# Sums of the first MLP weights' blocks: accumulating DMAs in DRAM in place of additions on VectorE

## The chip, the cores and the metric

The kernel runs on one core of a Trainium2 chip. The core has five engines, each with a queue of its own: TensorE (PE in the profile, with PEld for its weight loads), VectorE (DVE), ScalarE (ACT), GpSimd (POOL) and SyncE (SP). Transfers (DMAs) are issued from the queues of SP, ACT and POOL and are carried out by 16 DMA engines that all of them share. The metric is the device time of one execution in microseconds. The kernel before takes 1538.17 us, the median of three runs (1535.3 to 1539.74).

## The reference

The reference is one inference step of a backbone of two layers over 640 tokens: 512 latent tokens (`x_sample`) and 128 context tokens (`x_prompt`), of width 1024. All is float32. Each layer is

```
shift1, scale1, gate1, shift2, scale2, gate2 = split(mod)      # mod = silu(c) @ w_ada[l] + b_ada[l]
y = mixer(rmsnorm(x, norm1) * (1 + scale1) + shift1)           # one input projection, four head groups, one output projection
x = x + gate1 * y
h = rmsnorm(x, norm2) * (1 + scale2) + shift2
x = x + gate2 * (square(relu(h @ w1)) @ w2)                    # w1: 1024 x 4096, w2: 4096 x 1024
```

The four head groups are a short gated convolution, a chunked spatial-gating MLP, a latent attention and a windowed attention with sinks. A last RMSNorm ends it. The outputs are both groups of tokens and the context tokens' new cache entries of each layer. The change concerns `h @ w1` of the second layer.

## The kernel before

**Layout.** The activations lie feature-major in `x` (128 partitions, 8 k-tiles, 640 tokens). Tokens are worked on in two halves of 384 and 256 columns (`HALVES`). A weight arrives as a unit of 128 x 1024 float32 (512 KB) in a buffer of the pool `raw` (three buffers); ScalarE casts it to a high half and VectorE subtracts to get the low half, both in one tile `hl` (four buffers). `mm3` (L248 to L250) makes each product from three matmuls: high by high, high by low, low by high. `load_unit` (L235 to L240) is this sequence; with `pool=True` POOL makes the low half, which is used in layer 0's first projections and for the first four MLP units.

**Start.** `first_modulate` (L302) loads x from ScalarE's queue (four DMAs, L133) and natural-layout parts of `w_ada` as `adan` from SP's queue: eight tiles at L311 and, after these are used, four at L327. It ends with `late_consts`, which loads `vec` of layer 1 and `fn` (L143, L144). A `Norm` adds up squares, has POOL raise them to the power -1/2 (L295), and the result scales x. The rest of `w_ada` is streamed as `adaw` (`ada_tile`, L168 to L174) between other work through the whole of layer 0; the products with the conditioning vectors are made on VectorE.

**Mixer.** `tm_block` makes three token-major projections from units `raw<-in_wt`. The cached keys `cc` (L620) are loaded in the code behind all three. POOL's part in the mixer is the power of the row norms (L482) and the scaling of attention probabilities (L731, L968).

**MLP of layer 0.** 32 units of w1 and 32 of w2. `two_plain(j)` (L1232) makes four 128-row tiles of the hidden layer: per unit and half, 24 matmuls, a ReLU on ScalarE into `rr`, a square into `u`, a second square on POOL into `rq` (L1145), and on VectorE the low half of `u` (L1146). The buffers of `rr` and `rq` are five of the pool `pp` in all; the results of PE go through four single PSUM banks (`bank`). `mlp2(j)` (L1251) then multiplies by the w2 units, 12 matmuls per tile and half, and `gate_add` (L428) adds into x. The loop runs j = 0 to 7, `two_plain(j + 1)` ahead of `mlp2(j)`. After each unit of `mlp2` comes one `ada_steps(1)` as long as there are `adaw` tiles left.

**MLP of layer 1.** Here `h @ w1` is made by blocks (`Pair`): the units are taken in pairs, and for each pair a 2 x 2 block product of seven multiplications takes the place of eight. Pairs 0 and 1 are done plainly. For pairs 2 to 15, `full(p)` (L1223) calls `load` (L1149 to L1153), which fetches the two raw units r1 and r2 on SP's queue; `w1` splits r1; `w2` (L1163 to L1173) first makes four sums of blocks on VectorE, of 128 x 512 elements each, into the tiles `s23` and `s14` (tag `s`, two buffers in the pool `me`), and splits those and the last block of r2:

```
nc.vector.tensor_add(s14[:, 0], r2[:, 0], r2[:, 1])       # L1167
nc.vector.tensor_add(s23[:, 0], r1[:, 0], s14[:, 0])      # L1168
nc.vector.tensor_add(s23[:, 1], r1[:, 0], r2[:, 0])       # L1169
nc.vector.tensor_add(s14[:, 1], r1[:, 1], s23[:, 0])      # L1170
```

`first` and `rest` make the seven products (PSUM tiles `qa`, `qb`, `qcd`), each four blocks of three matmuls of 320 columns. The loop alternates `full` twice with one `mlp2`.

**Order.** The code is written as a sequence of tile operations. A planner orders each engine's queue when the program is built: an instruction may be placed ahead of earlier ones in the code if its operands, its buffers and its engine are free by the planner's own estimate of times. Once built, each queue runs strictly in order, and an instruction that waits holds everything behind it on its queue. The planner also sets all waits on semaphores.

Of the kernel before, what the change touches and what calls it, by code (L numbers as in the profile page):

```python
# [10 lines left out]
F32 = mybir.dt.float32  # L11
# [3 lines left out]
ALU = mybir.AluOpType  # L15
# [30 lines left out]
U_W1 = 9  # L46
# [10 lines left out]
def step_kernel(ctx, tc, xT, wf, wt, wt3, wo1, wo2, wq, wkvs, wada, wnat, wnat2, vec, rows, fnorm, cvec, cache, kpec,  # L57
                masks, rope_s, rope_q, rope_k, o_y, o_ckv, o_kpe, o_k, o_v):
    nc = tc.nc
# [11 lines left out]
    s2 = ctx.enter_context(tc.tile_pool(name="s2", bufs=2, space=PSUM))  # L71
# [9 lines left out]

    def close_phase():
        phase.pop("stack").close()

    uid = [0]

    def nm(s):
        uid[0] += 1
        return f"{s}_{uid[0]}"
# [9 lines left out]
    def bank2(s="bk2"):  # L99
        return s2.tile([128, 2, 512], F32, tag="s2", name=nm(s))  # L100
# [4 lines left out]
    def tb(shape, s, dt=F32R):  # L105
        return pool_b.tile(shape, dt, tag="b", name=nm(s))
# [10 lines left out]
    def tmp2(shape, s):  # L117
        return t2.tile(shape, F32, tag="t2", name=nm(s))
# [49 lines left out]
    def ada_tile(l, ct, pool=None):  # L168

        raw = pool([128, D], "adaw", F32) if pool else rawp.tile([128, D], F32, tag="raw", name=nm("adaw"))  # L170
        nc.sync.dma_start(out=raw, in_=wada[l, ct])
        junk = bank2("junk").rearrange("p a b -> p (a b)")
        for g in range(2):
            nc.vector.tensor_tensor_reduce(  # L174
                out=raw if g else junk, in0=raw, in1=cb[:, g, :], op0=ALU.mult, op1=ALU.add, scale=1.0,
                scalar=vecs[l][:, V_BADA + ct:V_BADA + ct + 1], accum_out=mods[l][g][:, ct:ct + 1])
        v, k = divmod(ct, KT)
        if v in (1, 4):
            gain(l, v // 4, k, 1)

    def gain(l, n, k, w):
        base, c0 = (V_N1, V_N2)[n], (KT, 4 * KT)[n] + k
        for g in range(2):
            nc.vector.scalar_tensor_tensor(
                out=gains[l][g][n][:, k:k + w], in0=mods[l][g][:, c0:c0 + w], scalar=1.0,
                in1=vecs[l][:, base + k:base + k + w], op0=ALU.add, op1=ALU.mult)

    class AdaRows:
# [6 lines left out]
        def step(self, k, raw):  # L195
            w = 128 * self.nk
            for v in range(2):
                nc.tensor.matmul(self.ps[0:2, v, :], lhsT=cs[:, :, k], rhs=raw[:, w * v:w * v + w],
                                 start=(k == 0 and (v == 0 or self.nk == 4)),
                                 stop=(k == KT - 1 and (v == 1 or self.nk == 4)))  # L200
# [27 lines left out]
    def ada_steps(n, pool=None):  # L228
        for _ in range(n):
            t = next(ada_it, None)  # L230
            if t is not None:
                ada_tile(*t, pool)


    def load_unit(src, n=1024, pool=False):  # L235
        raw = rawp.tile([128, 1024], F32, tag="raw", name=nm("raw"))
        nc.sync.dma_start(out=raw[:, :n], in_=src)
        hl = hlp.tile([128, 2, 1024], F32R, tag="hl", name=nm("hl"))
        nc.scalar.copy(hl[:, 0, :n], raw[:, :n])  # L239
        (nc.gpsimd if pool else nc.vector).tensor_sub(hl[:, 1, :n], raw[:, :n], f(hl[:, 0, :n]))  # L240
        return hl
# [15 lines left out]
    class Norm:  # L257
# [6 lines left out]
        def add(self, k, t0, n, pool=False):  # L264
            if k == 0:
                nc.scalar.activation(self.s[:, t0:t0 + n], x[:, k, t0:t0 + n], AF.Square)
                return
            sq = tmp2([128, 384], "sq")
            nc.scalar.activation(sq[:, :n], x[:, k, t0:t0 + n], AF.Square)  # L269
            (nc.gpsimd if pool else nc.vector).tensor_add(self.s[:, t0:t0 + n], self.s[:, t0:t0 + n], sq[:, :n])  # L270
# [165 lines left out]
    def layer(l, h, next_norm, nxt):  # L436
# [138 lines left out]
        ws = load_unit(wkvs[l, :, 512:1024], 512)  # L575
        wsH, wsL = (ws[:, s, 0:512].rearrange("p (h q) -> p h q", h=4) for s in range(2))
        for hd in range(4):
# [5 lines left out]
                out=u_t[:, :, d0:d0 + 64], in0=ps[:, :320].rearrange("p (t d) -> p t d", t=5),  # L583
# [501 lines left out]
        blocks = l == DEPTH - 1  # L1085
# [29 lines left out]
        me = phase.get("me")  # L1115

        class Pair:
# [5 lines left out]
            def __init__(self, p, u=None):  # L1123
                self.p = p
                pool = (lambda: me.tile([128, 2, TOK], F32R, tag="u", bufs=2, name=nm("u"))) if p % 3 == 0 \
                    else (lambda: tb([128, 2, TOK], "u"))
                self.u = u or [pool(), pool()]
                self.r, self.q = [None] * 2, [None] * 2
# [19 lines left out]
            def load(self):  # L1148
                self.raw = []  # L1149
                for i in range(2):  # L1150
                    raw = rawp.tile([128, 2, 512], F32, tag="raw", name=nm("raw"))
                    nc.sync.dma_start(out=raw, in_=wf[l, U_W1 + 2 * self.p + i].rearrange("p (a b) -> p a b", a=2))
                    self.raw.append(raw)  # L1153

            def hl(self, src, n=2):
                t = hlp.tile([128, 2, 2, 512], F32R, tag="hl", name=nm("hl"))
                split(t[:, 0, :n], t[:, 1, :n], src)
                return t
# [2 lines left out]
                self.wa = self.hl(self.raw[0])  # L1161

            def w2(self):  # L1163
                r1, r2 = self.raw
                s23 = me.tile([128, 2, 512], F32, tag="s", bufs=2, name=nm("s"))
                s14 = me.tile([128, 2, 512], F32, tag="s", bufs=2, name=nm("s"))
                nc.vector.tensor_add(s14[:, 0], r2[:, 0], r2[:, 1])  # L1167
                nc.vector.tensor_add(s23[:, 0], r1[:, 0], s14[:, 0])  # L1168
                nc.vector.tensor_add(s23[:, 1], r1[:, 0], r2[:, 0])  # L1169
                nc.vector.tensor_add(s14[:, 1], r1[:, 1], s23[:, 0])  # L1170
                self.ws23 = self.hl(s23)
                self.ws14 = self.hl(s14)
                self.w22 = self.hl(r2[:, 1:2], 1)  # L1173

            def mul(self, ps, w, i, op, start):
                for s in range(4):
# [74 lines left out]
        def mlp2(j, ut):  # L1251
            if j < 7:
                for i in range(4):
                    u = load_unit(wf[l, U_W2 + 4 * j + i])
                    for m in (2 * i, 2 * i + 1):
                        for half in range(2):
                            mlp2_tile(ut, u, m, half, None)
                    if l == 0:
                        ada_steps(1)
            else:  # L1260
                us = [load_unit(wf[l, U_W2 + 4 * j + i]) for i in range(4)]
                for m in range(8):
                    mlp2_tile(ut, us[m // 2], m, 0, next_norm)
                for m in range(8):
                    mlp2_tile(ut, us[m // 2], m, 1, next_norm)
                    if m >= 2:
                        nxt.step(0, m - 2)
                for half, k in ((0, 6), (0, 7)) + tuple((1, k) for k in range(KT)):
                    nxt.step(half, k)

        head = [Pair(p, None if blocks else [ta([128, 2, TOK], "u") for _ in range(2)]) for p in range(2)]
        ws = [load_unit(wf[l, U_W1 + i], pool=True) for i in range(4)]
# [181 lines left out]
```

## Time and profile before

| | |
|---|---|
| median of three runs | 1538.17 us (1535.3 to 1539.74) |
| profiled execution: device time, span | 1542.1 us, 1540.2 us |
| PE, PEld busy | 1477.7 us, 1418.2 us |
| DVE, ACT, POOL busy | 1129.9, 668.4, 242.9 us |
| mean granted clock of PE | 0.978 |
| DMA, mean over the span | 104 GB/s (160.22 MB) |

The span runs from the first to the last instruction of one profiled execution; its device time is a little longer. A busy time is the sum of an engine's instructions with overlaps counted once; a busy share is the average of stages that differ. The granted clock is given as a share of the full 2.4 GHz.

### The profile page before, as it was taken

The numbers are of one execution on the slowest core, as the hardware profiler recorded it, in microseconds if no ns is written. First come the engines' busy times: TensorE is split into PE (matmuls) and PEld (weight loads), VectorE is DVE, ScalarE is ACT, GpSimd is POOL, SyncE is SP. The second block draws the span as 40 slices with busy tenths as digits, with TensorE's granted clock in tenths as the row PEclk, the third lists the DMA queues.
The fourth block names the chain that finished last, engine by engine and source line by source line (L and its number), as shares of the span: only waits on it lengthen the run. The fifth ranks groups of instructions, "written<-read, shape, count | busy, mean of one in ns | idle before, by whom it ended". The sixth has DMA issues, their size and how long they took to land.

```text
span 1540.2 us, 25201 instructions
## 1 busy us (share of the span) xinstructions
PE 1477.7 (96%) x9716; PEld 1418.2 (92%) x9716; DVE 1129.9 (73%) x2210; ACT 668.4 (43%) x1400; POOL 242.9 (16%) x245
## 2 busy tenths in 40 slices
PE   6899999989999999999999999999999999999997
PEld 3798988889999999999999989898999999999996
DVE  5988877869978778776457666687886676566655
ACT  3544556744322322322236545675745244334422
POOL 2132103243210110110120120132300000000002
PEclk9899999999999999999999999999999999999999
DMA  8544321333654445444211411111223223222211
GB/s 312 202 134 139 99 67 35 102 101 100 204 161 155 151 139 163 151 150 138 80 49 57 128 43 35 36 49 45 83 69 96 69 83 96 62 76 96 84 55 69
DMA packets 50103, 160.22 MB, mean 104 GB/s; under 512 B 6208, under 2 KB 10304, under 8 KB 49984
## 3 DMA queue, kind: packets, MB, share of 16 engines
q1 hardware_dynamic: 48320, 154.68, 31.3%
q10 hardware_dynamic: 1664, 3.93, 0.7%
q8 instruction: 77, 1.26, 0.3%
q14 instruction: 42, 0.34, 0.1%
HBM read 155.55 MB, written 3.05 MB: 103 GB/s over the span
## 4 chain that ended last, share of the span: by engine, by line
PE 77%; DVE 10%; ACT 5%; issue 3%; POOL 1%; DMA 1%; POOLq 0%; DVEq 0%; ACTq 0%
PE w L250 13%; PE w L249 13%; PE w L248 13%; PE qcd L248 2%; PE fm L248 2%; PE qcd L250 2%; PE qcd L249 2%; PE fm L250 2%; PE fm L249 2%; PE out L248 2%; PE tm L249 2%; PE tm L248 2%; PE tm L250 2%; PE out L250 2%; PE out L249 2%
## 5 line engine op out<-in xcount | busy, mean ns | idle before, releaser
L248 PE MATMUL w<-u,hl 128*128 128x384 f32 (+1 forms) x1024 | 317.4, 310 | 5.7 <-DVE x L428 3.4
L249 PE MATMUL w<-u,hl 128*128 128x384 f32 (+1 forms) x1024 | 317.3, 310 | 0.7 <-DVE u L1198 0.7
L250 PE MATMUL w<-u,hl 128*128 128x384 f32 (+1 forms) x1024 | 317.1, 310 | 0.4 <-DVE hl L240 0.4
L239 ACT CAST hl<-raw 128x1024 fp32r<-128x1024 f32 (+3 forms) x176 | 170.6, 972 | 261.7 <-PE w L250 156.2
L240 DVE TENSOR_TENSOR hl<-raw,hl 128x1024 fp32r<-128x1024 f32 (+3 forms) x156 | 183.2, 1177 | 53.0 <-ACT hl L239 52.4
L428 DVE SCALAR_TENSOR_TENSOR x<-w,mod,x 128x128 f32<-128x128 f32 (+1 forms) x384 | 155.0, 434 | 73.1 <-PE w L250 71.8
L248 PEld LDWEIGHTS w<-u,hl 128*128 128x128 f32 x1024 | 194.6, 190 | 6.5 <-DVE x L428 3.6
L249 PEld LDWEIGHTS w<-u,hl 128*128 128x128 f32 x1024 | 194.8, 190 | 1.0 <-DVE u L1198 1.0
L250 PEld LDWEIGHTS w<-u,hl 128*128 128x128 f32 x1024 | 194.6, 190 | 0.6 <-DVE hl L240 0.6
L249 PE MATMUL w<-h,hl 128*128 128x384 f32 (+1 forms) x576 | 179.2, 313 | 3.6 <-DVE h L369 3.6
L250 PE MATMUL w<-h,hl 128*128 128x384 f32 (+1 forms) x576 | 179.4, 312 | 0.0
L248 PE MATMUL w<-h,hl 128*128 128x384 f32 (+1 forms) x576 | 179.0, 312 | 0.0
L174 DVE CUSTOM_DVE_ANT_0 junk<-adaw,cb,vec 128x1024 f32<-128x1024 f32 x84 | 110.5, 1317 | 28.2 <-DMA adaw<-in_wada 28.0
L270 POOL TENSOR_TENSOR ss<-ss,sq 128x384 f32<-128x384 f32 (+1 forms) x40 | 37.3, 932 | 504.7 <-ACT sq L269 503.9
L174 DVE CUSTOM_DVE_ANT_0 adaw<-adaw,cb,vec 128x1024 f32<-128x1024 f32 x84 | 114.2, 1359 | 1.1
L249 PEld LDWEIGHTS w<-h,hl 128*128 128x128 f32 x576 | 110.3, 192 | 4.8 <-DVE h L369 4.8
L1145 POOL TENSOR_TENSOR rq<-rr 128x384 f32<-128x384 f32 (+1 forms) x64 | 61.9, 969 | 334.2 <-ACT rr L1140 310.3
L248 PEld LDWEIGHTS w<-h,hl 128*128 128x128 f32 x576 | 110.5, 192 | 0.0
L250 PEld LDWEIGHTS w<-h,hl 128*128 128x128 f32 x576 | 110.3, 192 | 0.0
L248 PE MATMUL fm<-h,hl 128*128 128x256 f32 (+1 forms) x288 | 93.4, 324 | 2.1 <-DVE u L582 2.1
L249 PE MATMUL fm<-h,hl 128*128 128x256 f32 (+1 forms) x288 | 90.7, 315 | 0.0
L250 PE MATMUL fm<-h,hl 128*128 128x256 f32 (+1 forms) x288 | 90.6, 315 | 0.0
(329 smaller groups left out, 3404.6 us busy)
## 6 DMA issues: line engine op xcount, KB each, us to landing
raw<-in_wf SPq DMA_DIRECT2D x146, 512.0 KB, 3.5
adaw<-in_wada SPq DMA_DIRECT2D x84, 512.0 KB, 3.6
raw<-in_wo SPq DMA_DIRECT2D x24, 384.0 KB, 3.0
adan<-in_wnat SPq DMA_DIRECT2D x12, 512.0 KB, 8.3
raw<-in_wt SPq DMA_DIRECT2D x16, 384.0 KB, 3.3
x<-in_xT ACTq DMA_DIRECT2D x4, 640.0 KB, 7.2
raw<-in_wt SPq DMA_DIRECT2D x8, 288.0 KB, 3.0
raw<-in_wo SPq DMA_DIRECT2D x4, 512.0 KB, 3.6
```

Of the source, the lines that this page charges most:

```text
L174: nc.vector.tensor_tensor_reduce(out=raw if g else junk, in0=raw, in1=cb[:, g, :], op0=ALU.mult, op1=ALU.add, scale=1.0, scalar=vecs[l][:, ...
L239: nc.scalar.copy(hl[:, 0, :n], raw[:, :n])
L240: (nc.gpsimd if pool else nc.vector).tensor_sub(hl[:, 1, :n], raw[:, :n], f(hl[:, 0, :n]))
L248: nc.tensor.matmul(out, lhsT=lhs[0], rhs=rhs[0], start=start, stop=False, skip_group_check=more)
L249: nc.tensor.matmul(out, lhsT=lhs[0], rhs=rhs[1], start=False, stop=False, skip_group_check=more)
L250: nc.tensor.matmul(out, lhsT=lhs[1], rhs=rhs[0], start=False, stop=stop, skip_group_check=more)
L270: (nc.gpsimd if pool else nc.vector).tensor_add(self.s[:, t0:t0 + n], self.s[:, t0:t0 + n], sq[:, :n])
L428: nc.vector.scalar_tensor_tensor(out=x[:, m, t0:t0 + n], in0=ps[:, t0 - b0:t0 - b0 + n], scalar=mods[l][g][:, gate + m:gate + m + 1], in1= ...
L1145: nc.gpsimd.tensor_mul(q, r, r)
```

## The change

A class `WeightSums` makes the four sums of each pair in DRAM. Seven chunks of two pairs each (pairs 2 to 15) get two DRAM tiles, `ws23` and `ws14`. For a chunk, four plain DMAs from ScalarE's queue copy blocks of the weights into the tiles (lag 0), and four accumulating DMAs from POOL's queue add blocks or finished sums to them, one step later each (lags 1 to 3). Each of these 56 DMAs carries two blocks of 128 x 512, 512 KB. `step` is called behind each unit of `mlp2` in layer 0 from j = 4 on: 12 calls, of which ten have something to do. `Pair.load` in layer 1 then fetches the whole of r1, only the second half of r2, and the two sums into the `s` tiles, all on SP's queue; the four `tensor_add` of `w2` go.

```diff
+    dram = ctx.enter_context(tc.tile_pool(name="ws", bufs=1, space=bass.MemoryType.DRAM))
...
+    class WeightSums:
+        def __init__(self, l, c0, n):
+            self.l, self.c0, self.n, self.t = l, c0, n, 0
+            self.s23 = {}
+            self.s14 = {}
+
+        def of(self, p):
+            c, i = divmod(p, 2)
+            return self.s23[c][i], self.s14[c][i]
+
+        def step(self):
+            def blocks(c):
+                u = U_W1 + 4 * c
+                w = wf[self.l, u:u + 4].rearrange("(p i) q (a b) -> i a p q b", i=2, a=2)
+                return w[0, 0], w[0, 1], w[1, 0], w[1, 1]
+
+            def add(out, src):
+                nc.gpsimd.dma_start(out=out, in_=src, accum_op=ALU.add)
+
+            t = self.t
+            self.t += 1
+            for lag in (3, 2, 1, 0):
+                c = self.c0 + t - lag
+                if not self.c0 <= c < self.c0 + self.n:
+                    continue
+                a11, a12, a21, a22 = blocks(c)
+                if lag == 0:
+                    self.s23[c] = dram.tile([2, 128, 2, 512], F32, name=nm("ws23"))
+                    self.s14[c] = dram.tile([2, 128, 2, 512], F32, name=nm("ws14"))
+                s2, s3 = (self.s23[c][:, :, z, :] for z in range(2))
+                s1, s4 = (self.s14[c][:, :, z, :] for z in range(2))
+                if lag == 0:
+                    for out, src in ((s1, a21), (s3, a11), (s2, a11), (s4, a12)):
+                        nc.scalar.dma_start(out=out, in_=src)
+                elif lag == 1:
+                    add(s1, a22)
+                    add(s3, a21)
+                elif lag == 2:
+                    add(s2, s1)
+                else:
+                    add(s4, s2)
+
+    wsums = {1: WeightSums(1, 1, 7)}
...
@@ class Pair: def load(self) @@
-                    nc.sync.dma_start(out=raw, in_=wf[l, U_W1 + 2 * self.p + i].rearrange("p (a b) -> p a b", a=2))
+                    w = wf[l, U_W1 + 2 * self.p + i].rearrange("p (a b) -> p a b", a=2)
+                    nc.sync.dma_start(out=raw[:, i:], in_=w[:, i:])
                     self.raw.append(raw)
+                self.s = []
+                for src in wsums[l].of(self.p):
+                    t = me.tile([128, 2, 512], F32, tag="s", bufs=2, name=nm("s"))
+                    nc.sync.dma_start(out=t, in_=src)
+                    self.s.append(t)
...
             def w2(self):
-                r1, r2 = self.raw
-                s23 = me.tile([128, 2, 512], F32, tag="s", bufs=2, name=nm("s"))
-                s14 = me.tile([128, 2, 512], F32, tag="s", bufs=2, name=nm("s"))
-                nc.vector.tensor_add(s14[:, 0], r2[:, 0], r2[:, 1])
-                nc.vector.tensor_add(s23[:, 0], r1[:, 0], s14[:, 0])
-                nc.vector.tensor_add(s23[:, 1], r1[:, 0], r2[:, 0])
-                nc.vector.tensor_add(s14[:, 1], r1[:, 1], s23[:, 0])
+                s23, s14 = self.s
                 self.ws23 = self.hl(s23)
                 self.ws14 = self.hl(s14)
-                self.w22 = self.hl(r2[:, 1:2], 1)
+                self.w22 = self.hl(self.raw[1][:, 1:2], 1)
...
@@ def mlp2(j, ut): in the loop over i @@
                     if l == 0:
                         ada_steps(1)
+                        if 4 * j + i >= 16:
+                            wsums[1].step()
```

## Rows read from the trace of the kernel before

**Rows 1.** The page's first two parts, whole span

```profile
span 1540.2 us, 25201 instructions
...
PE 1477.7 (96%) x9716; PEld 1418.2 (92%) x9716; DVE 1129.9 (73%) x2210; ACT 668.4 (43%) x1400; POOL 242.9 (16%) x245
...
PEclk9899999999999999999999999999999999999999
DMA  8544321333654445444211411111223223222211
```

**Rows 2.** Windows: start:end, length, busy PE, PEld, DVE, ACT, POOL, clock, DMA, GB/s

```profile
0.00:20.00 20.00, 9.71 (x53) 9.22 (x54) 7.22 (x20) 9.99 (x23) 2.27 (x9) 0.93 0.93 360
20.00:120.00 100.00, 87.04 (x448) 67.66 (x446) 88.00 (x152) 46.23 (x119) 30.11 (x17) 0.93 0.54 183
...
640.00:670.00 30.00, 30.00 (x205) 30.00 (x204) 26.39 (x55) 4.35 (x5) 0.00 (x0) 1.00 0.45 143
...
1240.00:1293.00 53.00, 53.00 (x361) 52.62 (x360) 34.83 (x58) 20.57 (x28) 0.00 (x0) 1.00 0.26 80
```

**Rows 3.** Chain of waits, layer 1's MLP: start, length, what

```profile
1229.09 0.31 PE qcd L248
...
1282.27 0.31 PE qcd L248
```

**Rows 4.** Timeline of POOL, layer 0's MLP: start, length, instruction, idle before it

```profile
615.24 0.83 POOL L1145 TENSOR_TENSOR rq<-rr 128x384 f32<-128x384 f32 x1 [31.40 <-ACT rr L1140]
...
671.48 0.83 POOL L1145 TENSOR_TENSOR rq<-rr 128x384 f32<-128x384 f32 x1 [31.81 <-ACT rr L1140]
...
727.72 0.83 POOL L1145 TENSOR_TENSOR rq<-rr 128x384 f32<-128x384 f32 x1 [31.81 <-ACT rr L1140]
```

**Rows 5.** Groups by line, layer 1's MLP: count, busy us, mean ns, idle before

```profile
L248 PEld LDWEIGHTS qcd<-h,hl 128*128 128x128 f32 x112 | 21.0, 188 | 2.9 <-DVE rr L1213 1.1 <-DVE rr L1215 0.2
...
L1167 DVE TENSOR_TENSOR s<-raw 128x512 f32<-128x512 f32 x14 | 9.6, 688 | 2.1 <-DMA raw<-in_wf 2.0
...
L1170 DVE TENSOR_TENSOR s<-raw,s 128x512 f32<-128x512 f32 x14 | 9.5, 681 | 0.0
```

**Rows 6.** Who waited for whom, layer 1's MLP: us in total, times, longest

```profile
ACT hl L253 <- PE w L250: 132.8, 27, 6.0
...
DVE s L1167 <- DMA raw<-in_wf: 2.0, 3, 1.2
```

**Rows 7.** DMA issues over the span: count, KB each, us from issue to landing

```profile
raw<-in_wf SPq DMA_DIRECT2D x146, 512.0 KB, 3.5
...
adan<-in_wnat SPq DMA_DIRECT2D x12, 512.0 KB, 8.3
...
cs<-in_cvec SPq DMA_DIRECT2D x1, 8.0 KB, 2.6
```

**Rows 8.** Timeline of SP's queue, start of the kernel

```profile
13.70 0.33 SPq L143 DMA_DIRECT2D vec<-in_vec  x1
14.98 0.33 SPq L144 DMA_DIRECT2D fn<-in_fnorm  x1
...
38.56 3.96 SPq L327 DMA_DIRECT2D adan<-in_wnat  x4
...
53.55 0.65 SPq L620 DMA_DIRECT2D cc<-in_cache  x1
```

**Rows 9.** Waits of SP's queue in 0 to 60 us; ScalarE's queue, timeline

```profile
SPq L311 <- DMA x<-in_xT: 1.7, 1, 1.7
...
SPq L143 <- DMA adan<-in_wnat: 1.0, 1, 1.0
...
3.38 0.33 ACTq L133 DMA_DIRECT2D x<-in_xT  x1
```

**Rows 10.** Timeline of POOL, start of the kernel

```profile
16.53 1.55 POOL L295 TENSOR_TENSOR nst<-nst,mhalf 128x3 f32<-128x3 f32 x2 [15.23 <-DVE nst L293]
25.10 6.79 POOL L240 TENSOR_TENSOR hl<-raw,hl 128x768 fp32r<-128x768 f32 x3 [7.02 <-ACT hl L239]
```

## The prediction

> **What bounds the kernel now.** Read the page's first two parts before anything else. The span is 1540.2 us, and TensorE (PE) is busy for 1477.7 us of it, at a granted clock that is full in nearly every slice [rows 1]. So only work that feeds PE late can move the time. The windows by stage come next. In layer 1's MLP, where the removed additions run, PE is busy for all 53.00 us of a stretch of 53 us, at clock 1.00, while VectorE (DVE) is busy for 34.8 and the DMA engines for 0.26. In layer 0's MLP PE is full too (30.00 of 30 us), with the DMA engines at 0.45. The start is different: in the first 20 us PE is busy for 9.7 us and the DMA engines are 0.93 full, and from 20 to 120 us PE has 87 of 100 us with the DMA engines at 0.54 [rows 2]. There the loads set the pace.
>
> Is there something to win in layer 1's MLP? The chain of waits passes the same matmul of two successive rounds at 1229.09 and 1282.27: 53.18 us for 360 matmuls (two pairs of 7 x 12, and 192 of the second product), 147.7 ns each [rows 3]. In layer 0 the POOL multiplications recur every 56.24 us, for 384 matmuls of the same mean width: 146.5 ns [rows 4]. The two differ by 1.2 ns, so a round of layer 1 loses at most 360 x 1.2 = 0.45 us to everything that holds PE, and seven rounds lose 3 us.
>
> **The change part by part.** The profiled run took 1542.1 us, 1.9 more than its span; that is 3.9 above the median of 1538.2. I add to 1542.1 and take 3.9 off at the end.
>
> *Removed:* four additions in each of 14 pairs, 688 to 681 ns each [rows 5], 56 x 0.68 = 38 us of VectorE. They lie beside a full PE. PE's weight loads waited 2.9 us in all before the product that needs VectorE's sums, 1.3 us of it put down to VectorE [rows 5]. Gain: between 0 and 3 us; I take 1, the row nearest to it. What is late next is PE itself.
>
> *Loads in layer 1:* a pair fetches two sums of 512 KB and 256 KB less of the raw blocks, 0.75 MB more. At the 387 GB/s of the first 20 us (360 at a share of 0.93 [rows 2]) that is 2 us of DMA engines in 26.6 us, on a share of 0.26. The casts that read them are held by PE giving back the hl buffers, 132.8 us in all, whereas the waits for raw blocks sum to 2.0 us [rows 6]. Each s buffer comes free one pair ahead of its next use. Cost 0; without this cover it would be one landing of 3.5 us [rows 7] in each of 14 pairs, 49 us.
>
> *The new transfers:* seven chunks, each of four plain copies from ScalarE's (ACT) queue and four accumulating ones from POOL's: 28 and 28, each 512 KB within DRAM. No row shows such a transfer. A plain load of that size takes 1.35 us of all engines (0.524 MB at 387 GB/s) or 1.65 us by the rate of layer 0's MLP (143 GB/s at 0.45, so 318). An accumulating transfer may cost the same, or twice that, since it fetches two operands: 28 copies 38 to 46 us, 28 additions 38 to 92 us of engines.
>
> *When they run.* The copies read only an input and write DRAM that nothing else uses, so nothing holds them back to layer 0's MLP. The planner issues such transfers early. The loads of vec, fn and cc, written behind the whole first modulation (cc even behind three projections), go out at 13.70, 14.98 and 53.55 us, while the second adan loads, written earlier, wait for a buffer until 38.56 [rows 8]. I expect the copies at the front of ScalarE's queue, behind the four loads of x, in the stretch where PE waits for loads.
>
> Transfers of different queues also wait for one another there. SyncE's (SP) load of adan waits 1.7 us for a load of x that ScalarE issued, and vec 1.0 us for adan, though they share no data [rows 9]. The fourth load of x goes out only at 3.38 us [rows 9], when cs, one of the first transfers, has just had its 2.6 us to landing [rows 7]; I read this as a fixed number in flight over both queues. So the copies take places from the loads. If the two alternate, 28 copies pass together with 28 loads, 56 x 1.35 = 76 us, and what the loads had moved by then is 14.7 MB. Before, the loads had moved 7.2 MB in 20 us and went on at 183 GB/s [rows 2], which makes 14.7 MB at 20 + 7.5/0.183 = 61 us; all loads are late by 15 us at the end of that stretch. Bounds: 0 (copies placed behind the loads) and 46 us (all ahead of them). I take 15.
>
> *POOL.* A waiting addition holds POOL's queue, and behind it stand the norm's power (16.53 us), the weights' low halves of layer 0's projections (25.10 on, 6.79 us for three) and later the attention's scalings [rows 10]; PE waits for all of these. The order is fixed in advance, so each wait that lasts longer than planned is passed on. Bounds: 0 (POOL is busy only 30 of 100 us, and additions may fall into its gaps [rows 2]) and 28 x 8.3 = 232 us (each one waiting out a landing as long as adan's at the start [rows 7]). I take one ordinary landing of 3.5 us [rows 7] per chunk, for the two copies that the chunk's first additions wait for: 7 x 3.5 = 24.5 us. POOL also writes out these transfers; no row shows that, and I put it within the same bounds.
>
> *ScalarE's issue* of 28 copies: 0.33 us each by the row of the fourth x load [rows 9], 9 us beside gaps of an engine that is busy 46 of 100 us. Cost 0 to 9 us; I take 0.
>
> Sum: 1542.1 - 1 + 15 + 24.5 = 1580.6; less 3.9, **1577 us**. Its own range takes 0 to 46 for the loads and about 10 to 60 for POOL: 1548 to 1640.
>
> **The rivals.** *Program place.* The transfers stay in layer 0's last MLP rounds. POOL's multiplications of the round at 727.72 then stand behind the additions of the step before [rows 4]. Their waits need 28 copies and 21 additions, 49 transfers; with 0.55 of the engines free, one per 1.65/0.55 = 3.0 us, that ends 147 us after the first step at 640, at 787. PE can run on for six half tiles (five rr/rq buffers hold three results, four PSUM banks four more), 6 x 56.24/16 = 21 us, to 749. So 38 us are lost: 1542.1 + 38 - 1 - 3.9 = 1575. For it: the steps are written there. Against: rows 8.
>
> *Two engines.* The blocks' outermost dimension is 2. If a transfer is shared out by it, it runs on two of 16 engines: 0.524 MB at 387/16 x 2 = 48 GB/s is 10.8 us, and at 318 it is 13.2. The 28 copies from one queue then last 300 to 370 us, and each addition that the planner set too early holds POOL until its own. If POOL stands for half of that, 150 to 185 us are lost, at full length 300 to 370: 1542 + 168 - 4 = 1706 typically, 1908 at worst. If the planner reckons with it, nothing is lost but the loads' share on two engines. Against it in the profile: nothing, as every row here has the 128 partitions outermost.
> The Trainium skill ("DMA: Bandwidth & Descriptors", section "Rules for kernel authors", row "Use all 16 engines") states just this: an outermost dimension below 16 confines the transfer to at most that many engines. By that rule the sum is this rival's, and no run here shows it.
>
> *Hidden.* The additions fall into POOL's gaps and the copies behind the loads; what remains is the gain: 1533 to 1540, typically 1537, not slower. It decides for this if POOL never waits longer than planned and fewer than about four loads of the start are overtaken (4 x 1.35 = 5 us). For it: 1540 us of DMA engines with a low mean share, and sums needed only from about 1130 us on. Against: rows 9.
>
> **How the numbers follow.** A measurement of this kernel tells 0.3%, 4.6 us, from no change. Forecast (early, 1577) 0.40; program place (1575) 0.12; two engines (about 1706) 0.23; hidden 0.25, of which 0.05 is faster by over 4.6 us, which the bound of 3 us hardly allows, and 0.20 within it. Slower takes 0.40 + 0.12 + 0.23 = 0.75, of which some 0.03 would stay within 4.6 us. That gives 0.05, 0.23, 0.72. The range reaches from the hidden case's 1535 to 1740, past the typical case of two engines; outside stay its long half (0.10 to 0.12) and 0.03 below.
>
> **What would show it.** Early copies: ScalarE's queue shows 28 DMA issues ahead of 100 us, and first loads that land later than 8.3 us. Program place: they stand after 610 us, and PE has a gap near 749. Two engines: the copies take over 10 us each, with the mean DMA share low. POOL's hold: POOL's waits name DMA on the new tiles, ahead of L240, L482 or L1145. Layer 1's rounds should last 52.7 to 53.2 us. The prediction is wrong if PE has no new gap ahead of 1100 us, or if layer 1's MLP waits for the s tiles.

## The result and the profile after

The changed kernel took 1821.7 us (median of 4; 1819.9 to 1822.2) against 1538.7 us for the kernel before on the same chip: a ratio of 1.1833, 95% interval 1.1806 to 1.1861. The forecast was 1577 us with a range of 1535 to 1740; the sign was right, the size far off. One execution of a kernel below (k16) ran at a granted clock of 0.594 throughout and took 2418.3 us; its median leaves that one out.

The page's first three parts of the changed kernel; the counterparts are [rows 1]:

```profile
span 1820.4 us, 25325 instructions
...
PE 1537.5 (84%) x9716; PEld 1464.6 (80%) x9716; DVE 1101.2 (60%) x2154; ACT 667.4 (37%) x1400; POOL 280.0 (15%) x273
...
PEclk7679686876679899999999999999999999999999
DMA  6354565333433245454444212211121333333221
...
q0 software_dynamic: 32704, 14.88, 5.8%
q10 hardware_dynamic: 8888, 18.61, 2.7%
```

TensorE executes the same 9716 matmuls; they are busy for 59.8 us longer, as the granted clock is low in the first third (0.64 to 0.78 in the windows below, between the levels of 1.2 and 2.4 GHz), where PE has gaps. VectorE has 56 instructions fewer, the removed additions. The DMA engines are nowhere near full: the new queue q0 (POOL's, the 28 accumulating transfers) fills 5.8% of them and q10 (ScalarE's) 2.7%. A DMA share adds up the times of packets, so it can pass 1.

The windows (columns as in [rows 2]) say where the time went:

```profile
0.00:20.00 20.00, 5.73 (x32) 5.57 (x32) 2.83 (x9) 7.20 (x16) 0.73 (x7) 0.95 0.93 358
20.00:120.00 100.00, 29.75 (x96) 10.84 (x96) 36.88 (x65) 9.29 (x16) 14.33 (x9) 0.64 0.47 142
120.00:340.00 220.00, 145.42 (x729) 134.48 (x730) 99.42 (x202) 60.96 (x165) 49.71 (x41) 0.78 0.51 128
340.00:620.00 280.00, 184.14 (x1018) 164.65 (x1018) 133.61 (x301) 100.78 (x248) 59.28 (x55) 0.76 0.36 90
620.00:1100.00 480.00, 473.38 (x3185) 471.55 (x3185) 365.00 (x652) 142.49 (x245) 83.09 (x82) 0.99 0.42 134
```

From 20 to 120 us PE has 29.8 us of work instead of 87.0 [rows 2]; up to 620 us it stays starved, with a DMA share of 0.36 to 0.51. From 620 us on it is full again. The POOL multiplications of layer 0's MLP fix the border. The first and the last in the trace of before, then here:

```profile
358.98 0.83 POOL L1145 TENSOR_TENSOR rq<-rr 128x384 f32<-128x384 f32 x1 [2.93 <-ACT rr L1140]
...
751.53 0.61 POOL L1145 TENSOR_TENSOR rq<-rr 128x256 f32<-128x256 f32 x1 [1.93 <-ACT rr L1140]
...
639.46 0.83 POOL L1195 TENSOR_TENSOR rq<-rr 128x384 f32<-128x384 f32 x1 [3.06 <-ACT rr L1190]
...
1032.07 0.62 POOL L1195 TENSOR_TENSOR rq<-rr 128x256 f32<-128x256 f32 x1 [1.93 <-ACT rr L1190]
```

The first is 280.5 us late, and so is the last. So the whole loss lies ahead of layer 0's MLP, in the start and layer 0's mixer, and none where the additions are written (that MLP's last rounds) or where the sums are used: in layer 1's MLP the matmul of [rows 3] recurs every 53.2 us, as before.

```profile
1456.49 0.30 PE qcd L298
...
1509.68 0.30 PE qcd L298
```

Who held it, in 0 to 640 us (us in total, times, longest):

```profile
POOL ws L257 <- DMA ws<-in_wf: 291.8, 20, 57.5
POOL ws L257 <- DMA ws<-ws: 81.6, 6, 16.6
...
SPq L287 <- DMA ws<-in_wf: 46.6, 3, 26.0
```

L257 is the accumulating transfer, ws the sums in DRAM. POOL stands in front of them for 373 us in 26 waits: 241 us for ScalarE's copies (15 waits) and 132 for earlier additions (11). SP's load of weights (L287) waits for them as well. The chain of waits, 0 to 620 us, has "DMA ws<-in_wf 24.7%; issue 9.8%", together 214 us of 620 ("DMA ws<-ws" adds 2.4%); before, "issue" (time in which an engine waits for nothing that the profile shows) is 4.1% there and no such DMA exists. A stretch of it (start, length, what):

```profile
204.45 18.29 DMA ws<-in_wf
222.74 0.35 issue
223.08 31.54 DMA ws<-in_wf
254.62 0.29 issue
254.91 14.73 DMA ws<-ws
```

Three waits for transfers of 512 KB, 64.6 us, with next to nothing between. The page's list of DMA issues gives the median landings:

```profile
ws<-in_wf POOLq DMA_DIRECT2D x14, 512.0 KB, 27.7
ws<-ws POOLq DMA_DIRECT2D x14, 512.0 KB, 11.8
```

The copies on ScalarE's queue by the view of line 273 (length of the issue in ns, min/median/max; first and last start):

```profile
L273 ACTq DMA_DIRECT2D ws<-in_wf x28: 600/606/13678, 12.1 to 484.6; - x28
```

### The profile page after: what moved, and what is told of

Its sections match the earlier page's. It is cut to its first block, busy times and chain, and to the rows that moved or that the text cites. A ratio compares the mean times of both kernels' runs of the same rounds, so it can differ in the third digit from the quotient of the medians.

```text
span 1820.4 us, 25325 instructions
## 1 busy us (share of the span) xinstructions
PE 1537.5 (84%) x9716; PEld 1464.6 (80%) x9716; DVE 1101.2 (60%) x2154; ACT 667.4 (37%) x1400; POOL 280.0 (15%) x273
## 4 chain that ended last, share of the span: by engine, by line
PE 63%; DMA 11%; DVE 9%; issue 5%; ACT 4%; POOL 2%; ACTq 1%; POOLq 0%; DVEq 0%
PE w L300 11%; PE w L299 11%; PE w L298 11%; DMA ws<-in_wf 8%; PE qcd L298 2%; PE qcd L300 2%; PE qcd L299 2%; PE out L298 2%; PE fm L298 2%; PE out L300 2%; PE out L299 2%; PE fm L299 1%; PE fm L300 1%; DVE junk L176 1%; PE pt L294 1%
## 5 line engine op out<-in xcount | busy, mean ns | idle before, releaser
L176 DVE CUSTOM_DVE_ANT_0 junk<-adaw,cb,vec 128x1024 f32<-128x1024 f32 x84 | 116.1, 1383 | 74.6 <-DMA adaw<-in_wada 74.5
L1195 POOL TENSOR_TENSOR rq<-rr 128x384 f32<-128x384 f32 (+1 forms) x64 | 60.6, 947 | 335.7 <-ACT rr L1190 310.7
L298 PE MATMUL tm<-hl,h 128*128 128x384 f32 (+1 forms) x240 | 82.5, 345 | 34.7 <-ACT h L386 13.5
L298 PE MATMUL fm<-h,hl 128*128 128x256 f32 (+1 forms) x288 | 97.3, 338 | 9.3 <-ACT fr L681 4.8
L299 PE MATMUL fm<-h,hl 128*128 128x256 f32 (+1 forms) x288 | 93.9, 326 | 0.0
```

Source lines behind the costliest of these rows:

```text
L176: nc.vector.tensor_tensor_reduce(out=raw if g else junk, in0=raw, in1=cb[:, g, :], op0=ALU.mult, op1=ALU.add, scale=1.0, scalar=vecs[l][:, ...
L298: nc.tensor.matmul(out, lhsT=lhs[0], rhs=rhs[0], start=start, stop=False, skip_group_check=more)
L299: nc.tensor.matmul(out, lhsT=lhs[0], rhs=rhs[1], start=False, stop=False, skip_group_check=more)
L1195: nc.gpsimd.tensor_mul(q, r, r)
```

## The experiments

Theory at the start (A): a transfer with the blocks' pair outermost runs on two DMA engines, so it lasts over 10 us, and POOL and ScalarE, whose queues run in order, stand behind it in the mixer. Rivals: (B) place alone, the transfers are merely early; (C) accumulating transfers are dear in any shape; (D) the DMA engines' capacity.

### The transfers by themselves

One transfer after another, each writing the same half of a sums tile, nothing else running. `turn` puts the 128 partitions outermost:

```
for way in (same, turn):                      # from ScalarE; then from POOL with accum_op=add; then POOL without
    for n in range(4):
        nc.scalar.dma_start(out=way(d[:, :, 0, :]), in_=way(w[n // 2, n % 2]))
```

> The transfers alone, each waiting for the one before, with nothing else on the chip (the rest of the computation is left out): in this order 4 copies with the pair outermost and 4 with the 128 rows outermost from ScalarE's queue, then from POOL's queue 4 and 4 accumulating ones of the same two shapes, 4 and 4 plain ones, and 4 accumulating ones within the sums' own tiles. Theory 'two engines': with the pair outermost a 512 KB copy takes 11 to 14 us, with the 128 rows outermost 3 to 5 us, and the accumulating ones differ by the same factor. Rival 'slow in DRAM': copies of both shapes take 3 to 5 us, and it is the accumulating ones that take over 10 us in either shape.

From ScalarE's queue the chain shows

```profile
32.66 12.31 DMA wsd<-in_wf
...
57.20 3.63 DMA wsd<-in_wf
```

12.2 to 12.7 us with the pair outermost (the first 14.6), 3.6 with 128 outermost. From POOL's queue (L83 accumulates, L86 doesn't; the time in brackets is POOL's wait for the transfer before):

```profile
96.51 1.90 POOL L83 DMA_DIRECT2D wsd<-in_wf  x1 [22.45 <-DMA wsd<-in_wf]
121.06 1.87 POOL L83 DMA_DIRECT2D wsd<-in_wf  x1 [22.65 <-DMA wsd<-in_wf]
...
183.10 1.13 POOL L83 DMA_DIRECT2D wsd<-in_wf  x1 [5.04 <-DMA wsd<-in_wf]
189.27 1.14 POOL L83 DMA_DIRECT2D wsd<-in_wf  x1 [5.04 <-DMA wsd<-in_wf]
...
208.95 1.10 POOL L86 DMA_DIRECT2D wsd<-in_wf  x1 [12.13 <-DMA wsd<-in_wf]
222.99 1.06 POOL L86 DMA_DIRECT2D wsd<-in_wf  x1 [12.95 <-DMA wsd<-in_wf]
...
254.16 0.72 POOL L86 DMA_DIRECT2D wsd<-in_wf  x1 [3.14 <-DMA wsd<-in_wf]
258.11 0.69 POOL L86 DMA_DIRECT2D wsd<-in_wf  x1 [3.23 <-DMA wsd<-in_wf]
```

From start to start: accumulating 24.5 us (pair outermost) and 6.2 (128 outermost), plain 13.3 to 14.0 and 3.9. The additions from one sum to another (ws<-ws) took 5.5 to 7.6 us; the trace records their destination as [256,1] pieces of 2048 bytes where the narrow ones have [1,256], and they are not narrow. So rival C falls: additions are dear (below), but the shape is worth a factor of four to them too.

That "narrow" means two engines, the DMA share shows (length, busy DVE and POOL, clock, DMA share, GB/s), first beside the narrow copies, then beside the narrow additions:

```profile
20.00:50.00 30.00, 0.00 (x0) 0.00 (x0) 1.00 0.11 41
75.00:95.00 20.00, 0.00 (x0) 0.00 (x0) 1.00 0.18 26
```

Two of 16 engines are a share of 0.125. The packets recorded in the trace say the same: of a narrow copy two are under way nearly all the time, of one with 128 outermost 16 and more at its height, and a packet of 2048 bytes lasts 86 ns in the one and 95 in the other. So a narrow copy is long because its packets go two at a time, not because they are slower: 256 packets of 86 ns, two at a time, are 11.0 of its 12.3 us. In the narrow additions such a packet lasts 183 ns, which makes 23.4 of 24.5 us. Beside them go 7168 packets of 8 bytes (57 us in all, for four additions), which the additions with 128 outermost don't have and which put the share above 0.125. What they are for, no run shows.

The Trainium skill ("DMA: Bandwidth & Descriptors", section "Rules for kernel authors", row "Use all 16 engines") says that a transfer with an outermost dimension below 16 is kept to at most that many engines; the traces agree, 12.3 us against 3.6 and a share of 0.11.

So the change has 28 copies of 12.3 us and 14 additions of 24.5 us on two engines, and 14 more of about 6, each by itself.

### The shape, the place, and the removed additions

Three kernels beside one another: all transfers with 128 rows outermost (k16); the shape as changed but each step held behind a cast of layer 0's MLP (held2); no transfers at all, layer 1 loading other weight blocks in place of the sums (layer1_alone).

```
# k16
-   return w[0, 0], w[0, 1], w[1, 0], w[1, 1]
+   return [w[i, a].rearrange("p q b -> q p b") for i in range(2) for a in range(2)]
    (the same rearrange on s1, s2, s3, s4)
# held2
-   wsums[1].step()
+   with tc.issue_after(last_cast[0].ins):
+       wsums[1].step()
# layer1_alone
-   wsums[1].step()
-   for src in wsums[l].of(self.p):
+   for src in (two blocks of wf):
```

> The changed kernel with one edit: every block is walked with its 128 rows outermost and the pair second, in all 56 transfers; their number, bytes and place in the code are the same. Theory 'two engines' (the outermost dimension of 2 makes each transfer slow, and POOL's and ScalarE's queues stand behind it): POOL's waits for these transfers fall from 373 us to under 150 us, and the time to 1550 to 1640 us. Rivals 'slow in DRAM' (accumulating is slow in any shape) and 'place' (the early place is what costs, whatever the shape): it stays above 1700 us.

> The changed kernel with its transfers held to the place where the code has them: each step's copies are queued behind the cast of the unit loaded there, in layer 0's MLP; shapes as in the changed kernel. Rival 'place': there POOL and ScalarE have slack, the time falls to 1536 to 1560 us. Theory 'two engines': 28 copies still need some 11 us each one after another, and POOL's multiplications stand behind the additions; PE loses 100 to 250 us in layer 0's MLP, 1640 to 1790 us.

> Only layer 1's part: the four additions on VectorE go, the two s tiles are loaded in each pair, but from weight units that lie in DRAM anyway (so the sums are left out), and the 56 transfers are not issued. My step 'removed': 1 us gained, at most 3: 1535 to 1539 us. Rival 'new loads': if the s loads were late or held SyncE's queue it would be above 1545 us.

Measured: k16 1623.7 us, ratio 1.0530 [1.0494, 1.0565]; held2 1838.5, 1.1939 [1.1911, 1.1966]; layer1_alone 1538.5, 0.9986 [0.9967, 1.0004]. The shape alone is worth 198 of the 283 us, as theory A expected. Holding the transfers back with the shape left as it is saves nothing: rival B falls, though at 1838.5 us held2 also lost more than the 1790 that A allowed. (The forecast's price for the program place, 1575, was for transfers on all engines; held16 below is its test, at 1623 us.) The removal of the additions is worth nothing that can be measured: by layer1_alone's interval the new layer 1 wins at most about 0.3%.

In held2 the loss moved to the place where the transfers now run, and the line that carries it is another. The chain of waits of 640 to 1000 us, by line:

```profile
by line: ACTq L273 58.0%; issue 35.7%; DMA ws<-in_wf 11.6%; DMA adaw<-in_wada 2.0%; DMA raw<-in_wf 1.9%; ACT hl L290 1.4%; ACT rr L1191 0.5%; ACT u L1192 0.4%; DVE junk L176 0.4%; DVE adaw L176 0.4%; DVE hl L291 0.3%; DVE mod L176 0.0%; ACT
```

The window at its worst:

```profile
700.00:760.00 60.00, 9.07 (x48) 8.75 (x48) 6.04 (x13) 1.04 (x1) 6.16 (x5) 0.59 0.42 95
```

There ScalarE stands in the issue of its own copies: the 28 issues have a median of 12.1 us and go up to 31.8, about the length of a copy or of two or three, and the casts and activations behind wait. I read this as a queue that is full of long transfers and takes the next one only when one ends; no run tests that reading. PE gets 9 us of work in 60, where it had 60 before.

### Copies alone, and what 128 rows leave

```
# copies_only: add() does nothing           # held16: k16 and held2 together
-   nc.gpsimd.dma_start(..., accum_op=add)  # copies16: 128 rows outermost for the copies only
+   pass                                    # k16_again: k16 once more
```

> Both edits: 128 rows outermost in all 56 transfers, and the copies held behind the casts of layer 0's MLP. Theory 'two engines, then queues': a chunk's four additions still need 6.2 us each, one after another by their data, 28 x 6.2 = 174 us against some 150 us from the first step to the end of that MLP; POOL's multiplications have 21 us to spare per round, so the loss is small: 1540 to 1600 us. Rival 'any accumulating DMA in POOL's queue costs its whole landing': 1542 + 28 x 5 = 1680 us.

> The changed kernel without its 28 accumulating DMAs (the s tiles then hold the bare copies, the sums are left out): 28 copies on two engines at the early place. It parts ScalarE's queue and the slots in flight from POOL's queue. Theory 'POOL's queue': most of the 283 us goes, 1540 to 1640 us. Rival 'ScalarE's queue and slots': 28 copies x 12.6 us = 353 us still hold up loads and casts: above 1700 us.

> The changed kernel with the 128 rows outermost in the 28 copies alone; the accumulating DMAs keep the pair outermost. Theory 'POOL's queue': its 14 additions from the weights still take 24.4 us each, 342 us in all, and the time stays at 1700 to 1800 us. Rival 'ScalarE's copies are the cost': it falls to that of all 16-engine transfers, 1600 to 1640 us.

> The kernel with the 128 rows outermost once more, for a profile at the full clock: 1615 to 1630 us. Theory 'queues': of the 80 us that it is slower than the kernel before, most are POOL's waits for the sums' tiles ahead of layer 0's projections and attention, which PE then waits for. Rival 'loads': the DMA engines are full at the start and PE waits for adan and the units.

Measured: copies_only 1710.9, ratio 1.1101 [1.1066, 1.1136]; copies16 1823.9, 1.1843 [1.1804, 1.1883]; held16 1623.3, 1.0537 [1.0501, 1.0572]; k16_again 1625.7. The 28 narrow copies without any addition cost 170 us, so the copies are a cost by themselves and the expectation of most of the loss gone was wrong. With the copies on 128 rows and only the 14 additions narrow, the full 283 us stay (I had expected 1700 to 1800). These costs don't add up; my reading is that either holds the same mixer. In copies16 POOL's waits for the sums are only 40 us; there the loss shows as "issue" (15.8 us behind the addition at 512.56 us, 15.6 more behind POOL's next instruction), as waits of SP's queue (60.6 us of L287 for these transfers) and as later landings. I can't split it further.

What is left with all 16 engines, some 82 us, is the same early or held. Early, the engines are full (k16_again; PE had 77.9 and 96.3 us in these two windows before):

```profile
0.00:100.00 100.00, 52.09 (x186) 28.02 (x186) 49.81 (x83) 28.51 (x53) 22.46 (x24) 0.77 1.01 307
100.00:200.00 100.00, 54.92 (x304) 53.69 (x304) 37.92 (x84) 27.43 (x89) 35.54 (x29) 0.77 0.96 228
```

Held, they are full too, and PE had 60 of 60 us there before (held16):

```profile
640.00:700.00 60.00, 28.46 (x140) 27.16 (x139) 21.50 (x45) 5.00 (x6) 15.55 (x15) 0.66 1.01 238
700.00:760.00 60.00, 41.95 (x272) 40.64 (x271) 28.17 (x45) 12.32 (x21) 14.64 (x14) 0.87 1.05 260
```

held16 lies between its two expectations (up to 1600, or 1680). All this looked like rival D, and the next kernels tried it.

### Full engines, POOL's queue, or the loads' buffers

Three edits, each alone or with others, all on 128 rows outermost and held: layer 0's second square on ScalarE instead of POOL (`_act`), the ten steps spread over 28 units of the MLP in place of 12 (`spread16`), and, when a chain had named it, four buffers of their own for layer 1's modulation weights (`_aw`; adaw), which share three with the weight blocks.

```
# _act                                       # spread16
-   if blocks: nc.scalar.activation(q, r, Square)    -   if 4 * j + i >= 16:
-   else: nc.gpsimd.tensor_mul(q, r, r)              +   if (4 * j + i) % 3 == 0:
+   nc.scalar.activation(q, r, Square)
# _aw
+   def aw(shape, s, dt): return me.tile(shape, dt, tag="aw", bufs=4, name=nm(s))
-   ada_steps(1)
+   ada_steps(1, aw)
```

> As held16 (128 rows outermost, transfers held in layer 0's MLP; 1623 us), but layer 0's second square runs on ScalarE, so that POOL has no multiplication of the MLP standing behind a waiting addition. If the remaining 82 us come from POOL's queue being held, most of them go: 1545 to 1575 us. If they come from full DMA engines (133 us of all 16 engines asked for in about 150 us, beside the weights' loads at a share of 0.2 to 0.47), PE still waits for the weights and the time stays: 1610 to 1630 us, with the DMA share about 1 in 640 to 760 us.

> As held16, but the ten steps are spread over all 28 units of layer 0's second product (one every third unit, about 450 us in place of 150), POOL's multiplication as it was. The 133 us of engine time that the 56 transfers take then fit beside the loads (0.3 more on a share of 0.2 to 0.5). Theory of full engines: 1540 to 1560 us, no stretch with a DMA share near 1. Rival, each waiting addition holds POOL whatever the room: a step is still four additions behind a DMA, so 7 to 10 times some 8 us stay: 1600 to 1625 us.

> spread16 with layer 0's second square on ScalarE as well. If anything of spread16's loss is POOL's queue, it goes here: 1538 to 1545 us. If the loss is in the engines, it stays as in spread16 within 5 us. Removing VectorE's additions was worth nothing measurable, so neither theory gives less than 1534 us.

> As held2 (two engines per transfer, held in layer 0's MLP; 1838 us), with layer 0's second square on ScalarE. If the loss there is POOL standing for the additions (28 x 24.5 = 686 us of two engines), it shrinks to what the loads and ScalarE's issues cost: 1700 us or less. If it is ScalarE's own queue standing in its copies' issues (10 to 30 us each), it stays: 1800 to 1850 us, with ScalarE's issues as the largest share of the chain.

Measured: held16_act 1604.9, ratio 1.0414 [1.0380, 1.0448]; spread16 1620.6, 1.0508 [1.0464, 1.0551]; spread16_act 1601.9, 1.0395 [1.0362, 1.0428]; held2_act 1843.9, 1.1970 [1.1936, 1.2004]. spread16 refutes rival D in my form: the DMA share fell to 0.66 to 0.78 and the time stayed. held16_act and spread16_act came out between their two expectations: POOL's multiplications seemed to be worth only some 18 us. (held2_act's expectation counts 28 additions at 24.5 us; only 14 are narrow.) The chain of held16_act showed a third thing, 43.2% of 620 to 860 us:

```profile
668.04 10.96 DMA adaw<-in_wada
679.03 1.29 DVE junk L176
...
680.85 1.19 DVE adaw L176
...
683.73 11.17 DMA adaw<-in_wada
```

These modulation tiles land 11 us after their issue, against a median of 3.6 before (3.5 for a weight block of the same size [rows 7]); VectorE reduces each in two passes (junk, adaw), and only then is a buffer free for the next load. VectorE's queue stands meanwhile, with PE's inputs behind it. Hence the last kernels.

> spread16_act (1602 us) with four buffers of their own for the modulation weights (adaw) in layer 0's MLP, in place of the three that they share with the weight blocks. In spread16_act a reduction on VectorE ends, an adaw load starts, lands 3.4 to 10 us later (3.4 to 3.6 before), and the next reduction waits, 50 times, 143 us in all. Theory, few shared buffers turn longer landings into PE's loss: 1538 to 1555 us, with VectorE's waits for adaw below 40 us. Rival, the 16 engines can't deliver both (133 us more in about 340 us): 1590 to 1605 us.

> held16_act (1605 us) with the same four buffers. Here the transfers come within some 150 us and the DMA share was 0.96 to 1.00 from 640 to 760 us, so the engines are full whatever the buffers: by the theory of shared buffers at most a third of the 66 us goes, 1580 to 1605 us; should it fall to 1540 to 1560 us, the buffers alone were the loss even with full engines.

> Control: layer1_alone (no transfers between DRAM and DRAM at all, layer 1 loads other blocks in place of the sums; 1538 us) with the four buffers for adaw. PE is full in layer 0's MLP there, so by every theory 1533 to 1543 us, the same as before.

Measured: spread16_act_aw 1545.1, ratio 1.0022 [1.0000, 1.0044]; held16_act_aw 1542.2, 1.0007 [0.9986, 1.0027]; layer1_aw 1548.9, 1.0042 [1.0024, 1.0059]. The loss is gone, and my expectation for held16_act_aw (1580 to 1605) was wrong: the engines are as full as they were, and PE doesn't notice (held16_act_aw):

```profile
640.00:700.00 60.00, 60.00 (x412) 60.00 (x411) 24.02 (x43) 18.23 (x33) 9.19 (x8) 1.00 1.06 281
700.00:760.00 60.00, 60.00 (x413) 60.00 (x412) 26.68 (x46) 19.18 (x34) 12.65 (x11) 1.00 0.93 211
```

VectorE's wait for adaw over the whole span fell from 135.0 to 0.4 us. The control, at 1548.9 us just above its 1533 to 1543, costs 0.4% more than the kernel before, so the buffers themselves win nothing. The control for ScalarE's squares without transfers was not run, so a small gain there could hide a small loss.

Were it the buffers alone, POOL's multiplications could go back, and the narrow shape too:

> held16_act_aw (1542 us) with layer 0's second square back on POOL, where it stands behind waiting additions. Its floor is layer1_aw, 1549 us, which has the buffers and POOL's squares but no transfers. Theory, the three shared buffers were the loss and POOL adds its own: without the adaw waits, 1549 to 1575 us. Rival, POOL's queue alone explains what held16 lost: 1600 us or more, as in held16 (1623 us).

> held16_act_aw with the transfers as the change has them, the pair outermost (12.6 us a copy, 24.5 us an addition on two of 16 engines). held2 and held2_act took 1838 and 1844 us with ScalarE's issues as the largest part of the chain. Theory, ScalarE stands in the issues of its own copies whatever buffers the loads have: 1750 to 1850 us. Rival, the shared buffers were the loss there too: 1545 to 1620 us.

Measured: held16_aw 1617.0, ratio 1.0507 [1.0478, 1.0536]; held2_act_aw 1829.6, 1.1882 [1.1846, 1.1919]. Theory lost in the first and held in the second. With the buffers but with POOL's squares, nearly all the loss is back, now through POOL. In held16_aw VectorE waits for the squares (us in total, times, longest, 600 to 1100 us), and POOL's timeline shows why:

```profile
DVE u L1199 <- POOL rq L1198: 118.9, 15, 21.3
...
656.09 1.13 POOL L257 DMA_DIRECT2D ws<-ws  x1 [11.87 <-DMA ws<-ws]
656.81 1.27 POOL L1198 TENSOR_TENSOR rq<-rr 128x384 f32<-128x384 f32 x1
...
670.97 1.14 POOL L257 DMA_DIRECT2D ws<-ws  x1 [9.99 <-DMA ws<-in_wf]
671.68 1.28 POOL L1198 TENSOR_TENSOR rq<-rr 128x384 f32<-128x384 f32 x1
681.85 1.17 POOL L257 DMA_DIRECT2D ws<-ws  x1 [8.89 <-DMA ws<-ws]
682.61 1.06 POOL L1198 TENSOR_TENSOR rq<-rr 128x256 f32<-128x256 f32 x1
```

Each of the multiplications shown comes at once behind an addition that had waited 9 to 12 us for its operand. From 656 to 696 us there are four, where a round of 56.24 us [rows 4] takes eight, one every 7 us. So with 16 engines there are two holds side by side, and each alone keeps most of the loss (the first step, from 1623.3 to 1617.0, is within the noise of the two ratios, 1.0537 and 1.0507):

| 128 rows outermost, held | squares on POOL | squares on ScalarE |
|---|---|---|
| adaw in the shared buffers | 1623.3 | 1604.9 |
| adaw in four of its own | 1617.0 | 1542.2 |

The planner orders the queues anew for every kernel, and no run holds that order fixed while one edit is made, so the smaller differences can be partly its. In the early place (k16) I have not told the two apart; POOL waits there for 138 us for the sums. In held2_act_aw neither is left, but ScalarE stands in the issues of its copies (the next takes 12.03 us):

```profile
630.26 28.60 ACTq L273 DMA_DIRECT2D ws<-in_wf  x1
```

## Why the prediction was wrong, point by point

- **The price of a transfer.** The forecast costed every one of the 56 transfers at 1.35 to 1.65 us of all engines, additions up to twice that, from loads whose partitions stand outermost. Measured: 12.3 us for a copy and 24.5 for 14 of the additions, on two engines. This is the root: the step that failed is the sharing out over all 16 engines. With 128 rows outermost the price would have held for a copy (a DMA share of 0.42 over 14.6 us for four, 1.5 us of all engines each) and been too low for an addition (0.59 over 25.2 us for four, 3.7 each). The condition stood in the text as the rival "two engines", at 0.23, and nothing in the profile spoke against it; the diff's access patterns, which show a pair outermost, should have made it the likeliest. Its own price (1706, from copies of 10.8 to 13.2 us, which was right) was 116 us short: it left out that a narrow accumulating transfer takes twice as long as the narrow copy, and took it that POOL stands for half of the copies' length; copies16, with only the additions narrow, has the whole loss. Its 1908 for the full length was nearer than its typical case.
- **POOL: "7 x 3.5 = 24.5 us", one ordinary landing per chunk.** The term that failed by most. POOL waited 373 us in 26 waits, 14 us each and up to 57.5; nearly every addition waits, not one pair per chunk, in 20 waits for a narrow transfer and in 6 for another sum. The chain of 0 to 620 us has 168 us of waiting for these transfers (24.7% and 2.4%). Even the upper bound of 232 us was passed, as it took 8.3 us for the longest landing.
- **ScalarE's issue, 0 of 0 to 9 us.** Wrong in kind: an issue takes 0.6 us by itself, but much longer when long transfers stand ahead of it on its queue. Eight issues in the changed kernel took 10.7 to 13.7 us each; by themselves the narrow copies cost 170 us (copies_only), and held back they were the largest term (held2, held2_act_aw).
- **The loads 15 us late.** Not separable in the changed kernel: in the first 20 us the engines moved as much as before (358 against 360 GB/s), but PE did 5.7 us of work instead of 9.7, and adan landed after 9.4 us (8.3 [rows 7]). SP's waits for the sums fit the reading of [rows 9], a fixed number in flight over both queues, and the trace shows what it is: SP's and ScalarE's transfers report their landing on the same eight semaphores (100 and 102 to 108; POOL's on eight others, 111 to 118), and 22 of the 28 copies wait for the one that they will raise. So a transfer of 12 us keeps one of the eight from the loads for that long; how much time that cost is not shown.
- **Early.** Right in direction: the first copy goes out at 12.1 us though it is written in layer 0's last MLP rounds. But not "28 DMA issues ahead of 100 us": three are, and the last follows at 484.6. With 128 rows outermost in the copies all 28 are out by 80 us (copies16); why the narrow ones are not is not shown. Place was then no cause: held2 lost as much as the changed kernel, and held16 as much as k16.
- **The gain of 1 us and the loads of the sums at 0.** Right: layer1_alone is within 0.3%, the rounds still take 53.2 us, and the sums' loads, like the kernel's others, are hidden. Neither of the signs of being wrong that the prediction named came true, and it missed all the same: PE's new gaps lie ahead of 1100 us, and layer 1's MLP doesn't wait for the s tiles.
- **"Hidden" (0.25)** had the right reserve, but not for free: the sums can be made beside the work without a loss (held16_act_aw), if the transfers use all engines, POOL has nothing urgent behind them, and the loads have buffers for longer landings.
- Two sums are rounded loosely, without effect: 360 x 1.2 ns is 0.43 us, and the early case's own range is 1547 to 1643 by its terms.

## What to carry to other kernels

Read a new DMA's access pattern before its bytes: here a pair outermost meant two engines, and 12.3 against 3.6 us. Then ask, for every in-order queue that issues it, what stands behind an instruction that waits for a transfer and behind an issue that takes as long as one, and for every load beside it whether its buffers cover a landing three times as long. When one of two parallel holds is removed and little changes, remove both before either is acquitted: 18 us and 6 us alone (the 6 within the noise), 81 together.

## What the runs showed of the hardware

An accumulating transfer within DRAM of 512 KB takes 1.6 to 1.8 times a plain one from the same queue (6.2 against 3.9 us on all engines, 24.5 against 13.3 to 14.0 on two); its packets of 2048 bytes lasted 183 ns on two engines, where a plain copy's lasted 86. A ScalarE whose queue holds long transfers stood in the issue of the next, up to 31.8 us (held2), with its arithmetic behind it. And a DMA share near 1 did not by itself mean a starved PE: with 1.06 and 0.93 in two windows PE was full once its inputs were covered, and with 0.66 to 0.78 it wasn't when they were not.
